# Row sums on one core: the last 64 columns of five loads are sent by two small transfers each

## The chip, the cores and the metric

The kernel runs on one core of a Trainium2 chip; the other cores are idle. The metric is device time in microseconds, and the time of a kernel is the median of its runs. Before the change it was 161.3 us, the median of 3 runs from 161.15 to 161.41.

## What is computed

The input is 64 MiB of float32; each row of 1024 numbers becomes one number.

```python
def setup_inputs():
    batch, seq, dim = 32, 512, 1024
    return {"x": np.random.randn(batch, seq, dim).astype(np.float32)}

def reference(x):
    return np.sum(x, axis=-1).astype(np.float32)
```

## The kernel before

There are 16,384 rows, 128 for each of the 128 partitions of on-chip memory. The first 2,048 rows of the input form one view (`x_a`: partition p holds rows 16p to 16p+15), the other 14,336 another (`x_b`: 112 consecutive rows for each partition). `rows_from` (L131) picks rows `j` to `j+n` of every partition from the one or the other. In both views the rows of a partition are contiguous, so a load of 16 rows reads 64 KB in one stretch for each partition.

All loads are issued by SP (SyncE), in this order: the first 7 rows of `x_b` (L212); then seven whole loads of 16 rows (L214 to L224), of which the first is all of `x_a` and the others are rows 16 to 111 of `x_b`; then what is left of rows 0 to 15, as 6 rows, 2 rows and the last row in two parts of 560 and 464 columns (L227, L228, L236, L237). A load of 16 rows is 8 MiB. The pool `in` has three buffers, so a whole load is issued when the reduction three tiles before it has read its buffer. The first load is moved to the entry of the program, ahead of the start-up barrier; the first two whole loads are held back by explicit dependencies (L222, L224), the first until a small ScalarE instruction has run, the second until the first 7 rows are reduced.

VectorE reduces the first 7 rows and six of the seven whole loads with one instruction each, `tensor_reduce` over 16 rows (L152). The last whole load and the small loads behind it are worked off row by row, by VectorE (`halves`, L166: it adds the two halves of a row and accumulates) and by ScalarE (`act`, L179). The last row's two parts are added by two further `halves` instructions (L241, L242). The row sums gather in the tile `sums`; ScalarE's queue stores two parts of it when the loads are nearly through, and SP stores the last 16 columns at the end (L243).

The function `rows` (L188) issues one load and the instructions that reduce it; the change is made in it and in the loop over `wholes` (L215) that calls it. Each transfer reports its completion on one of eight counters that are used in turn.

Of the kernel before, what the change touches and what calls it, by code (L numbers as in the profile page):

```python
# [100 lines left out]
@with_exitstack  # L101
def kernel(
    ctx: ExitStack,
    tc: tile.TileContext,
    x: bass.AP,
    out: bass.AP,
):
    nc = tc.nc
    nc.at_finalize(issue_first_load_at_entry)
    nc.at_finalize(order_waits)  # L110
    nc.at_finalize(wait_for_the_store_at_the_clear)
    fp32 = mybir.dt.float32
    P = 128
    batch, seq, dim = x.shape
    rows = batch * seq
    J = rows // P
    BIG = 16

    LONG = J - BIG
    rows_in = x.flatten_outer_dims()
    rows_out = out.rearrange("b s -> (b s)")
    x_a = rows_in[: P * BIG].rearrange("(p j) d -> p j d", p=P)
    x_b = rows_in[P * BIG :].rearrange("(p j) d -> p j d", p=P)
    out_a = rows_out[: P * BIG].rearrange("(p j) -> p j", p=P)
    out_b = rows_out[P * BIG :].rearrange("(p j) -> p j", p=P)


    def rows_from(j, n):  # L131
        return x_b[:, j : j + n, :] if j < LONG else x_a[:, j - LONG : j - LONG + n, :]

    last = 0
    FIRST = 7
    pieces = (560, 464)
    LINE = 64

    with (
        tc.tile_pool(name="small", bufs=1) as smallpool,  # L140
        tc.tile_pool(name="in", bufs=3) as inpool,
        tc.tile_pool(name="unread", bufs=4, space=bass.MemoryType.PSUM) as upool,
        tc.tile_pool(name="stage", bufs=1) as stpool,
        tc.manual_schedule(),
    ):


        seed = smallpool.tile([P, LINE // 2], fp32)
        sums = stpool.tile([P, J], fp32)

        def vec(dst, src):
            return nc.vector.tensor_reduce(  # L152
                out=dst, in_=src, axis=mybir.AxisListType.X, op=mybir.AluOpType.add
            )

        def hold(inst, until, reason):
            tc.add_manual_dep(
                inst.ins,
                until.ins.name,
                mybir.DependencyInfo(mybir.DependencyClass.Sync, mybir.DependencyReason.DATA),  # L160
                reason=reason,
            )

        def halves(dst, src):
            n = src.shape[-1] // 2
            return nc.vector.tensor_tensor_reduce(  # L166
                out=src[:, :n],
                in0=src[:, :n],
                in1=src[:, n:],
                scale=1.0,  # L170
                scalar=0.0,
                op0=mybir.AluOpType.add,
                op1=mybir.AluOpType.add,
                accum_out=dst,
            )

        def act(dst, src, n):
            unread = upool.tile([P, dim], fp32)
            nc.scalar.activation(  # L179
                out=unread[:, :n],  # L180
                in_=src,
                func=mybir.ActivationFunctionType.Copy,
                accum_out=dst,
            )

        sums_of = []

        def rows(t, a, n, j, n_act, pairs=False):  # L188
            nv = n - n_act
            block = t[:, a * dim : (a + n) * dim].rearrange("p (n d) -> p n d", d=dim)  # L190
            load = nc.sync.dma_start(out=block, in_=rows_from(j, n))  # L191
            if pairs:
                for q in range(nv):
                    sums_of.append(halves(sums[:, j + q : j + q + 1], block[:, q, :]))
            else:
                sums_of.append(vec(sums[:, j : j + nv], block[:, :nv, :]))
            for q in range(nv, n):
                act(sums[:, j + q : j + q + 1], block[:, q, :], dim)
            return load

        def store(eng, dst, j0, j1):
            return eng.dma_start(out=dst, in_=sums[:, j0:j1])

        nc.vector.memset(seed[:, :1], 0.0)  # L204
        unread = upool.tile([P, dim], fp32)
        ready = nc.scalar.activation(  # L206
            out=unread[:, :1], in_=seed[:, :1], func=mybir.ActivationFunctionType.Copy
        )

        j = last  # L210
        t = inpool.tile([P, BIG * dim + LINE], fp32)
        rows(t, 0, FIRST, j, 0)  # L212
        first = sums_of[-1]
        wholes = [LONG, *range(BIG, LONG, BIG)]  # L214
        for k, at in enumerate(wholes):  # L215
            t = inpool.tile([P, BIG * dim + LINE], fp32)
            if k < len(wholes) - 1:
                load = rows(t, 0, BIG, at, 0)
            else:
                rows(t, 0, BIG, at, 7, pairs=True)  # L220
            if k == 0:
                hold(load, ready, "no second load while the first one's descriptors are made")  # L222
            if k == 1:
                hold(load, first, "no descriptors of later loads while the first ones start")  # L224

        t = inpool.tile([P, BIG * dim + LINE], fp32)
        rows(t, FIRST, 6, j + FIRST, 2, pairs=True)  # L227
        two = rows(t, FIRST + 6, 2, j + FIRST + 6, 1, pairs=True)  # L228
        a = BIG - 1

        j += a
        c, width = pieces
        whole = t[:, a * dim + c : BIG * dim + 2]
        nc.vector.memset(whole[:, width + 1 :], 0.0)  # L234
        part = t[:, a * dim : a * dim + c]
        nc.sync.dma_start(out=part, in_=rows_from(j, 1)[:, 0, :c])  # L236
        nc.sync.dma_start(out=whole[:, :width], in_=rows_from(j, 1)[:, 0, c:])  # L237
        late = "its packets come behind those of the loads"
        hold(store(nc.scalar, out_b[:, BIG:], BIG, LONG), two, late)
        hold(store(nc.scalar, out_a, LONG, J), two, late)  # L240
        halves(whole[:, width : width + 1], part)  # L241
        halves(sums[:, j : j + 1], whole)  # L242
        store(nc.sync, out_b[:, :BIG], 0, BIG)  # L243
# [30 lines left out]
```

## Time and profile before

| | |
|---|---|
| median of 3 runs | 161.3 us (161.15 to 161.41) |
| span of the profiled execution | 159.5 us |
| VectorE busy | 120.6 us, 76% of the span |
| of it `tensor_reduce` of 16 rows | 6 times 17.22 us |
| ScalarE busy | 12.1 us, 8% |
| read from HBM | 67.11 MB, 421 GB/s over the span |
| packets of the transfers | 2160, of which 624 under 512 bytes |
| SP's wait for reductions | 102.2 us |

The span goes from the first to the last instruction of one profiled execution; the device time of a run also holds what lies around it, here 1.8 us. In the rows of the profile, an engine's name stands beside the line of the kernel whose instruction ran (DVE is VectorE, ACT ScalarE, SP SyncE, SPq its queue of instructions). The transfers are carried out by 16 DMA engines, called queues below: each works off its share of the packets of a transfer in order. "DMA share" is their mean busy share, with each packet's time counted in the window in which the packet starts.

### The profile page before, as it was taken

How to read it: one execution, taken by the hardware profiler on the slowest of the kernel's cores; microseconds unless marked ns; L12 is line 12 of the kernel's file. 1: busy time of each engine (PE TensorE's matmuls, PEld its weight loads, DVE VectorE, ACT ScalarE, POOL GpSimd, SP SyncE). 2: the span in 40 equal slices, each digit the busy share in tenths (PEclk: the TensorE clock that was granted, in tenths of full speed). 3: DMA queues.
4: the chain of work that ended last, by engine and by line, in shares of the span. 5: the costliest groups of instructions: out<-in, count | busy, mean ns of one | idle time of the engine just before them, and what ended most of it. 6: DMA issues, size and time to landing. Idle time of an engine off the chain costs nothing.

```text
span 159.5 us, 135 instructions
## 1 busy us (share of the span) xinstructions
DVE 120.6 (76%) x41; ACT 12.1 (8%) x22; POOL 0.2 (0%) x4
## 2 busy tenths in 40 slices
DVE  0029600499995999769996899949999499994955
ACT  3000000000000000000000000000000000003993
POOL 0000000000000000000000000000000000000000
DMA  8899899699699699699699798996996996996993
GB/s 302 388 493 526 362 427 526 296 493 526 263 526 526 263 526 526 263 526 493 296 526 444 345 526 378 411 526 296 493 526 263 526 526 263 526 526 265 425 382 128
DMA packets 2160, 67.18 MB, mean 421 GB/s; under 512 B 624, under 2 KB 752, under 8 KB 880
## 3 DMA queue, kind: packets, MB, share of 16 engines
q1 hardware_dynamic: 1872, 67.12, 97.8%
q10 hardware_dynamic: 288, 0.06, 0.2%
HBM read 67.11 MB, written 0.07 MB: 421 GB/s over the span
## 4 chain that ended last, share of the span: by engine, by line
DMA 71%; DVE 27%; SPq 1%; issue 0%; DVEq 0%
DMA t<-in_x_dram 71%; DVE sums L152 26%; SPq L191 0%; SPq L236 0%; DVE t L166 0%; DVEq L269 0%
## 5 line engine op out<-in xcount | busy, mean ns | idle before, releaser
L152 DVE TENSOR_REDUCE sums<-t 128x16 f32<-128x16384 f32 (+1 forms) x7 | 110.9, 15849 | 32.3 <-DMA t<-in_x_dram 32.3
L179 ACT ACTIVATE unread<-t 128x1024 f32<-128x1024 f32 x10 | 10.1, 1011 | 144.3 <-DMA t<-in_x_dram 144.3
L166 DVE CUSTOM_DVE_ANT_0 t<-t 128x512 f32<-128x512 f32 (+2 forms) x16 | 9.6, 654 | 4.0 <-DMA t<-in_x_dram 4.0
L179 ACT ACTIVATION_READ_ACCUMULATOR unread<-t 128x1 f32 x10 | 1.9, 188 | 0.0
L206 ACT ACT_TABLE_LOAD x1 | 1.3, 1283 | 0.8 <-PEq L258 0.8
L166 DVE DVE_READ_ACCUMULATOR2_ANT sums<- 128x1 f32 x15 | 1.2, 82 | 0.0
L204 DVE MEMSET seed<- 128x1 f32 x1 | 0.1, 59 | 0.8 <-PEq L258 0.8
L206 ACT ACTIVATE unread<-seed 128x1 f32<-128x1 f32 x1 | 0.2, 174 | 0.0
L258 POOL MEMSET const-bfloat16-1.0<- 128x1 bf16 x1 | 0.1, 102 | 0.0
L258 POOL MEMSET const-uint8-127<- 128x1 uint8 x1 | 0.1, 102 | 0.0
L258 POOL MEMSET const-float32-0.0<- 128x1 f32 x1 | 0.1, 99 | 0.2 <-issue 0.2
L258 POOL MEMSET const-float32-1.0<- 128x1 f32 x1 | 0.1, 99 | 0.0
L166 DVE DVE_READ_ACCUMULATOR2_ANT t<- 128x1 f32 x1 | 0.1, 83 | 0.0
L234 DVE MEMSET t<- 128x1 f32 x1 | 0.1, 59 | 0.0
## 6 DMA issues: line engine op xcount, KB each, us to landing
t<-in_x_dram SPq DMA_DIRECT2D x1, 3584.0 KB, 11.0
t<-in_x_dram SPq DMA_DIRECT2D x1, 3072.0 KB, 28.7
t<-in_x_dram SPq DMA_DIRECT2D x1, 1024.0 KB, 30.7
t<-in_x_dram SPq DMA_DIRECT2D x1, 280.0 KB, 31.0
t<-in_x_dram SPq DMA_DIRECT2D x1, 232.0 KB, 31.1
t<-in_x_dram SPq DMA_DIRECT2D x7, 40.7
out_dram<-sums ACTq DMA_DIRECT2D x1, 48.0 KB, 1.6
out_dram<-sums ACTq DMA_DIRECT2D x1, 8.0 KB, 1.6
```

The costliest lines, as they stand in the source:

```text
L152: return nc.vector.tensor_reduce(out=dst, in_=src, axis=mybir.AxisListType.X, op=mybir.AluOpType.add)
L166: return nc.vector.tensor_tensor_reduce(out=src[:, :n], in0=src[:, :n], in1=src[:, n:], scale=1.0, scalar=0.0, op0=mybir.AluOpType.add, op ...
L179: nc.scalar.activation(out=unread[:, :n], in_=src, func=mybir.ActivationFunctionType.Copy, accum_out=dst,)
L204: nc.vector.memset(seed[:, :1], 0.0)
L206: ready = nc.scalar.activation(out=unread[:, :1], in_=seed[:, :1], func=mybir.ActivationFunctionType.Copy)
L234: nc.vector.memset(whole[:, width + 1 :], 0.0)
L258: nc = _bacc.Bacc("TRN2", target_bir_lowering=False, num_devices=1)
```

## The change

For five of the seven whole loads (the second to the sixth), the load itself ends 64 columns early: it takes 16,320 of the 16,384 columns of a partition. The last 64 columns, 256 bytes in each partition, are sent by two small transfers that SP issues right behind it: one over the first partitions (120, 126, 117, 108 and 119 of them) and one over the others (8, 2, 11, 20 and 9). The first and the last whole load and the loads of fewer rows are left as they were, and no instruction of VectorE or ScalarE is changed; a reduction of a cut load waits for three transfers in place of one.

```diff
+    EDGE = 64
...
-        def rows(t, a, n, j, n_act, pairs=False):
+        def rows(t, a, n, j, n_act, pairs=False, head=0):
             nv = n - n_act
             block = t[:, a * dim : (a + n) * dim].rearrange("p (n d) -> p n d", d=dim)
-            load = nc.sync.dma_start(out=block, in_=rows_from(j, n))
+            src = rows_from(j, n).rearrange("p n d -> p (n d)")
+            cut = n * dim - (EDGE if head else 0)
+            load = nc.sync.dma_start(out=t[:, a * dim : a * dim + cut], in_=src[:, :cut])
+            if head:
+                at = slice(a * dim + cut, (a + n) * dim)
+                nc.sync.dma_start(out=t[:head, at], in_=src[:head, cut:])
+                nc.sync.dma_start(out=t[head:, at], in_=src[head:, cut:])
...
         wholes = [LONG, *range(BIG, LONG, BIG)]
+        heads = {1: 120, 2: 126, 3: 117, 4: 108, 5: 119}
         for k, at in enumerate(wholes):
             t = inpool.tile([P, BIG * dim + LINE], fp32)
             if k < len(wholes) - 1:
-                load = rows(t, 0, BIG, at, 0)
+                load = rows(t, 0, BIG, at, 0, head=heads.get(k, 0))
```

## The prediction

> **What bounds the kernel now.** I read the chain of waits in order of time first, because it names what released each step. Its last part:
>
> ```profile
> 107.58 17.23 DVE sums L152
> ...
> 124.82 0.33 SPq L191
> ...
> 126.16 31.13 DMA t<-in_x_dram
> 157.30 0.02 issue
> 157.32 0.40 DVE t L166
> ```
>
> The columns are start, length and what ran. The end is set by the landing of the last piece of input at 157.30 us; behind it come a 0.40 us add and the last store, 2.19 us up to the end of the span at 159.49. The chain steps back from that landing to its issue, then to the reduction that freed the buffer; that is no proof of a wait that matters, for the load was asked for 31 us before it landed. So I asked next whether the transfers ever ran dry, with windows of one load each (last two columns: DMA share, GB/s):
>
> ```profile
> 69.00:88.30 19.30, 17.22 (x2) 0.00 (x0) 0.00 (x0) 1.00 1.00 435
> 88.30:107.60 19.30, 17.24 (x2) 0.00 (x0) 0.00 (x0) 1.00 1.00 435
> ```
>
> They don't: share 1.00, 435 GB/s, which is 27.2 bytes per ns for each of 16 queues. VectorE needs 17.22 of the 19.3 us of a load and waits the other 2.1. SP waits most of all, always to ask early:
>
> ```profile
> SPq L191 <- DVE sums L152: 102.2, 6, 17.2
> ```
>
> The kernel is bound by its transfers from 1.0 us to the end, and what counts is the queue that finishes last. How far apart the 16 queues run shows in narrow windows at the moments when each begins its first, and its forty-ninth, 64 KB packet; a packet counts where it starts, and 328 GB/s in 0.2 us is one packet:
>
> ```profile
> 9.90:10.10 0.20, 0.00 (x0) 0.00 (x0) 0.00 (x0) 1.00 0.76 328
> 10.10:10.30 0.20, 0.00 (x0) 0.00 (x0) 0.00 (x0) 1.00 4.55 1966
> 10.30:10.50 0.20, 0.00 (x0) 0.00 (x0) 0.00 (x0) 1.00 5.31 2294
> 10.50:10.70 0.20, 0.00 (x0) 0.00 (x0) 0.00 (x0) 1.00 1.52 655
> ...
> 125.90:126.10 0.20, 0.00 (x0) 0.00 (x0) 0.00 (x0) 1.00 0.77 328
> 126.10:126.30 0.20, 0.00 (x0) 0.00 (x0) 0.00 (x0) 1.00 4.59 1966
> 126.30:126.50 0.20, 0.00 (x0) 0.00 (x0) 0.00 (x0) 1.00 5.34 2294
> 126.50:126.70 0.20, 0.00 (x0) 0.00 (x0) 0.00 (x0) 1.00 1.52 655
> ```
>
> That is 1, 6, 7 and 2 packets, at 10 us and again 116 us later: each queue keeps the lateness it got at the start. The whole spread is some 0.5 to 0.6 us, and two queues come about 0.15 us behind the rest (a window from 10.46 to 10.62 us is empty). If the work were dealt out so that all ended together, the end could come about 0.25 us earlier (half the spread), as long as the dealing itself cost nothing.
>
> **Which queue gets what.** The edit takes 128 pieces of 256 bytes out of each of five loads and sends them as ten small transfers. Before, the page counts 2160 packets for 15 transfers: 15 x 128 of data and 15 x 16 of four bytes, so every transfer went in equal shares of 8 rows, with one closing packet each, to all 16 queues. 120, 8, 126, 2, 117, 11, 108, 20, 119 and 9 rows have no sixteenth. I assume that equal shares stay the rule, on the largest number of queues up to 16 that divides the rows, always from the first queue on: 15, 8, 14, 2, 13, 11, 12, 10, 7 and 9 queues. Added up over the five loads, the queues then carry, in place of 40 pieces each: 58, 58, 57, 57, 57, 57, 57, 40, 39, 38, 36, 35, 26, 17, 8 and 0. [...]
>
> **The price of a piece.** No 256-byte read is in the trace, so I bound it. Below: bytes alone, 256 / 27.2 = 9.4 ns. Above: the two stores that are made of small packets, read with windows on the queues alone:
>
> ```profile
> q1 hardware_dynamic: 144, 0.01, 10.3%
> ...
> q10 hardware_dynamic: 144, 0.05, 49.4%
> ```
>
> The first is 64-byte packets in a window of 0.90 us: 0.103 x 16 x 0.90 / 144 = 10.3 ns each. The second is 384-byte packets in 0.37 us: 0.494 x 16 x 0.37 / 144 = 20.3 ns. In between, 256 bytes come to 16.3 ns, and four bytes to 8.4. Neighbouring packets of a queue overlap a little: the page gives the loads' queue 97.8% of 16 x 159.5 us, 156.0 us a queue, and a queue has on average only from 1.1 to 156.7 us and a tenth more for the last store; 0.3 us over some 117 packets is 2 ns. I take 14.5 ns for a piece and 7 ns for a closing packet, between the bounds and near the upper rows.
>
> **The sum.** What a queue saves in the five loads is 40 x 9.4 = 376 ns. The five queues with 57 pieces pay 57 x 14.5 = 827 ns and ten closing packets, 70 ns: 521 ns more than before (at 9.4 ns and free closing packets, 160; at 16.3 and 8.4, 637). A queue with no piece gains 376. The latest of the seven loaded queues decides. Which queues are late the trace doesn't say; if the seven were drawn at random, one of the two late ones is among them with 1 - (9 x 8)/(16 x 15) = 0.70, and the end moves by 0.52 us; else by 0.15 less, 0.37. If the loaded ones are the seven earliest, some 0.35 us ahead of the last, it still moves by 0.17. Together about +0.5 us.
>
> **Costs I put at nothing.** Ten issues on SP, 0.33 to 0.44 us each by the rows of the loads' issues: SP is idle for them, and a load is asked for some 20 us before its queue needs it (asked 66.87, landed 107.55, its forerunner 88.3); without that cover they would add 0.7 us a load. The built order adds waits: completion counters come in a ring of eight, so with 25 transfers in place of 15 the second small transfer of the third, fourth and fifth cut load waits for the main part of a load two earlier to land, about 2 us after SP gets there. Behind it in SP's queue stands the next whole load, which waits for a reduction some 17 us later anyway. VectorE's reductions wait for three landings in place of one; SP's rows of such a wait are 17 ns each, inside VectorE's 2.1 us of idle. The instructions of VectorE and ScalarE and the last four loads are unchanged, so the 2.19 us behind the last landing stay, as do the 1.8 us between the span and the median. The profiled execution goes from 159.5 to 160.0 us, the median of 161.3 to 161.8.
>
> **Rivals.** *The late queues are relieved.* If the queues with few pieces are just those that set the end, and the loaded seven are over 0.9 us ahead of them (0.52 + 0.376), the end comes up to 0.376 us earlier: about 160.95. Against it: the windows show a spread of at most 0.6 us. For it: an unprofiled execution may start less evenly than this one. *Even dealing.* If any number of rows is spread over all 16 queues, each gets 40 pieces: 40 x 14.5 + 70 - 376 = +0.27 us, 161.57. The equal shares of before speak for neither. *Pieces in the way of others.* Until now each queue wrote only its own partitions. Shares of 17 rows or 9 fall elsewhere, and if a piece holds up the queue that owns the partition while it itself waits, each costs another 9.4 ns on the loaded queues: +0.52 + 57 x 9.4 ns = +1.05, 162.35. No view of before shows a transfer in another's way. [...] *It doesn't reach the end:* the pieces hide in gaps between packets that the records do not show; 161.3.
>
> **How the numbers follow.** Forecast 0.58 (own range 161.4 to 162.1), relief 0.12, even dealing 0.12, pieces in the way 0.13, no effect 0.05. Within 0.2% of before, which is 0.32 us and about what a measurement can tell from no change, lie 0.10 of the forecast, 0.07 of even dealing and 0.04 of no effect: 0.21. Faster is the relief alone, 0.12. The rest, 0.67, is slower. The range 161.2 to 162.3 leaves out the relief below and half of the collisions above, 0.18.
>
> **What would show it.** The packets: equal shares add 640 pieces and 15+8+14+2+13+11+12+10+7+9 = 101 closing packets, 2901 in all; even dealing adds 160 closing ones, 2960. The landing of the last piece should move from 157.30 to about 157.8, with VectorE's wait for it longer; narrow windows where the seventh whole load begins should show the 16 starts drawn out from 0.6 to about 1 us, some earlier than before, half of them later. A stretch below 430 GB/s in the middle of the loads would mean that a wait has emptied the queues, which I have excluded; a spread that shrinks would make the forecast wrong.

## The result and the profile after

The changed kernel takes 162.03 us (median of five runs) where the kernel before took 161.19 in the same comparison. The ratio is 1.0046 with a 95% interval of 1.0032 to 1.006, so the change costs 0.5 to 1.0 us. Three runs of this document were 2 to 3.5 us slower than the rest of their kernel: one of these five, at 165.44 us, which is left out of the ratio and of the spans below, and two of the twelve of `after_less` (an experiment below), at 163.66 and 163.87 us, which are in its ratio and widen its interval. The forecast was 161.8, in a range of 161.2 to 162.3.

The chain of waits of the changed kernel in order of time, its last part (start, length, what ran):

```profile
126.83 30.75 DMA t<-in_x_dram
157.58 0.04 issue
157.62 0.40 DVE t L167
```

The last piece lands at 157.58 us instead of 157.30. The span of this execution grows with it, from 159.5 to 159.8. That is only part of the loss. Each run has its device time and its span, and the part outside the span has grown as well: 2.13 to 2.17 us in every run of the changed kernel, 1.74 to 1.84 in every run of the kernel before that went with the experiments. The forecast had put the whole loss inside the span.

Inside the span things went as foreseen. The transfers did not run dry in the middle of the loads (windows of one load each; last two columns DMA share and GB/s):

```profile
69.00:88.30 19.30, 17.22 (x1) 0.00 (x0) 0.00 (x0) 1.00 1.01 435
88.30:107.60 19.30, 17.22 (x1) 0.00 (x0) 0.00 (x0) 1.00 1.01 435
```

The page's line on the packets, and below it the narrow windows where the queues begin their first 64 KB packet and where they begin the seventh whole load:

```profile
DMA packets 2901, 67.18 MB, mean 420 GB/s; under 512 B 1365, under 2 KB 1493, under 8 KB 1621
```

```profile
9.90:10.10 0.20, 0.00 (x0) 0.00 (x0) 0.00 (x0) 1.00 0.76 328
10.10:10.30 0.20, 0.00 (x0) 0.00 (x0) 0.00 (x0) 1.00 4.55 1966
10.30:10.50 0.20, 0.00 (x0) 0.00 (x0) 0.00 (x0) 1.00 6.07 2622
10.50:10.70 0.20, 0.00 (x0) 0.00 (x0) 0.00 (x0) 1.00 0.76 328
...
125.90:126.10 0.20, 0.00 (x0) 0.00 (x0) 0.00 (x0) 1.00 0.77 328
126.10:126.30 0.20, 0.00 (x0) 0.00 (x0) 0.00 (x0) 1.00 0.77 328
126.30:126.50 0.20, 0.00 (x0) 0.00 (x0) 0.00 (x0) 1.00 4.06 1697
126.50:126.70 0.20, 0.00 (x0) 0.00 (x0) 0.00 (x0) 1.00 4.87 2034
126.70:126.90 0.20, 0.00 (x0) 0.00 (x0) 0.00 (x0) 1.00 2.45 1020
```

2901 packets is the number that equal shares on as many queues as divide the rows give; even dealing would have made 2960. At 10 us the 16 queues start as 1, 6, 8 and 1 packets, close to the 1, 6, 7 and 2 of before. At 126 us one starts early and one 0.2 us later, some five start between 126.3 and 126.5, six between 126.5 and 126.7 and three behind 126.7 (256-byte pieces make up the odd GB/s). By the packets' own start times in the two traces, the 0.5 us in which all 16 start have become 0.84 us (126.05 to 126.89), where the kernel before still has 0.5: the uneven dealing pulled them apart.

VectorE's instructions for line 153, the reductions, show what else the edit added:

```profile
L153 DVE TENSOR_REDUCE sums<-t x7: 7619/17219/17220, 11.0 to 127.5; 128x16 f32<-128x16384 f32 x6, 128x7 f32<-128x7168 f32 x1
L153 DVEq EVENT_SEMAPHORE  x5: 49/50/50, 49.9 to 127.3; - x5
```

Each of the five reductions that wait for three landings is preceded by an instruction of its own that only waits, 50 ns each in VectorE's idle time. The kernel before has none of them at its reductions, so the list of VectorE's instructions has become longer by five. That matters for another reason than their 50 ns, as the experiments show.

### The profile page after: what moved, and what is told of

It is laid out like the page before. It is cut to its first block, busy times and chain, and to the rows that moved or that the text cites. A ratio compares the mean times of both kernels' runs of the same rounds, so it can differ in the third digit from the quotient of the medians.

```text
span 159.8 us, 151 instructions
## 1 busy us (share of the span) xinstructions
DVE 120.6 (75%) x41; ACT 12.1 (8%) x22; POOL 0.2 (0%) x4
## 2 busy tenths in 40 slices
DMA packets 2901, 67.18 MB, mean 420 GB/s; under 512 B 1365, under 2 KB 1493, under 8 KB 1621
## 4 chain that ended last, share of the span: by engine, by line
DMA 81%; DVE 16%; SPq 1%; issue 0%; DVEq 0%
DMA t<-in_x_dram 81%; DVE sums L153 16%; SPq L194 1%; SPq L197 0%; SPq L244 0%; DVE t L167 0%; SPq L198 0%; DVEq L153 0%; DVEq L277 0%
```

## The experiments

Twelve kernels ran, each at least five times, against the kernel before. The table has the medians: span, device time minus span ("outside"), device time, all in us; "VectorE" is how many instructions of VectorE its trace records more than the trace of the kernel before, which has 50. Each comparison's own runs of the kernel before had a median of 161.19 to 161.26; in the experiments their span was 159.4 to 159.5 and 1.76 to 1.79 us lay outside.

| kernel | pieces | VectorE | span | outside | time |
|---|---|---|---|---|---|
| changed kernel | 640, uneven | +5 | 159.85 | 2.15 | 162.03 |
| `e_even` | 640, even, ten transfers | +5 | 159.6 | 2.15 | 161.80 |
| `e_one` | 640, even, five transfers | +5 | 159.6 | 2.18 | 161.80 |
| `e_lump` | 640, on seven queues | +5 | 160.2 | 2.20 | 162.40 |
| `e_idle` | 10 | 0 | 159.4 | 1.78 | 161.23 |
| `e_wait` | 10 | +5 | 159.5 | 2.21 | 161.63 |
| `e_extra` | 640 on top, even | 0 | 160.0 | 1.77 | 161.76 |
| `e_pad` | none | +5 | 159.8 | 2.18 | 161.97 |
| `e_less` | none | -6 | 159.4 | 1.78 | 161.21 |
| `e_pad1` | none | +1 | 159.6 | 1.78 | 161.38 |
| `e_pad15` | none | +15 | 159.8 | 1.79 | 161.62 |
| `after_less` | 640, uneven | -1 | 159.75 | 1.78 | 161.54 |
| `after_pad35` | 640, uneven | +40 | 160.5 | 1.81 | 162.31 |

### Is it the dealing, or the program?

The first theory after the result, A, was that the queues cost about half and a longer program of SP, with ten transfers more to issue, the rest. The rival, B, left everything to the queues. Four kernels went together.

`e_even` deals the same pieces evenly:

```diff
-        heads = {1: 120, 2: 126, 3: 117, 4: 108, 5: 119}
+        heads = {1: 112, 2: 112, 3: 112, 4: 112, 5: 112}
```

> All five cut loads send their 640 pieces as 112+16 rows, so that every one of the 16 queues gets 40 of them, with as many transfers (ten) as the changed kernel. Theory A (the loss is half in the queues, half in a longer program): the span grows by 40 x 14.1 ns + 10 x 6 ns - 376 ns = 0.25 us to about 159.75, the time outside the span stays at the changed kernel's 2.15 us, median about 161.9. Theory B (the whole loss comes from the queues that carry 57 pieces): even dealing gives back most of it, median about 161.4.

Measured: 161.80 us, 1.0041 of before (1.0027 to 1.0055), span 159.6, outside 2.15. The 14.1 ns for a piece and 6 ns for a closing packet, here and in what follows, fit the records of the changed kernel's trace: 18 and 9 ns, less the 3 to 4 ns by which neighbouring packets of a queue overlap there. (In the kernel before, too: a whole load is eight packets of 2.419 us and one of 9 ns for a queue, 19.36 us by their records, and the first packets of two loads start 19.33 us apart.) In the span even dealing gives back most of the loss (0.25 of 0.4 us); outside it, nothing. The windows at the seventh whole load of this kernel:

```profile
126.10:126.30 0.20, 0.00 (x0) 0.00 (x0) 0.00 (x0) 1.00 0.19 39
126.30:126.50 0.20, 0.00 (x0) 0.00 (x0) 0.00 (x0) 1.00 7.21 3026
126.50:126.70 0.20, 0.00 (x0) 0.00 (x0) 0.00 (x0) 1.00 5.55 2343
126.70:126.90 0.20, 0.00 (x0) 0.00 (x0) 0.00 (x0) 1.00 0.00 0
```

All 16 queues start within 0.4 us: nothing has pulled them apart.

`e_lump` makes the dealing more uneven:

```diff
-        heads = {1: 120, 2: 126, 3: 117, 4: 108, 5: 119}
+        heads = {1: 119, 2: 119, 3: 119, 4: 119, 5: 119}
```

> All five cut loads are 119+9, so that seven queues get 90 pieces each, two get five and seven get none; ten transfers. Both theories: the seven queues carry 90 x 14.1 + 10 x 6 - 376 = 0.95 us more than before (57 pieces: 0.49), so the last landing comes 0.4 to 0.5 us later than in the changed kernel: span 160.2 to 160.4, median 162.4 to 162.6. If the dealing doesn't set the end, the median stays at 162.0. The count of packets is 2160 + 640 + 5 x (7 + 9) = 2880.

Measured: 162.40 us, 1.0071 (1.0058 to 1.0084), span 160.2, outside 2.20, 2880 packets. The span is 0.35 us longer than the changed kernel's, at the low end of what was expected. Its windows, 0.4 us wide, in which 164 GB/s is one packet:

```profile
125.70:126.10 0.40, 0.08 (x1) 0.00 (x0) 0.00 (x0) 1.00 3.09 1312
126.10:126.50 0.40, 0.00 (x0) 0.00 (x0) 0.00 (x0) 1.00 0.39 164
126.50:126.90 0.40, 0.00 (x0) 0.00 (x0) 0.00 (x0) 1.00 0.04 8
126.90:127.30 0.40, 0.00 (x0) 0.00 (x0) 0.00 (x0) 1.00 1.43 555
127.30:127.70 0.40, 0.00 (x0) 0.00 (x0) 0.00 (x0) 1.00 1.56 665
```

Nine queues begin the load by 126.5, then none for 0.4 us, then seven: 119 rows went to seven queues, in five loads running always to the same seven. For 119 rows this shows what the forecast had to assume. The packets agree with it in sum: 2901 in the changed kernel, 2880 here and 2960 in `e_even`. Which seven of the sixteen queues it is no record here shows. The nine also show that relief is real: eight of them start before 126.1, where in the kernel before only one did.

`e_one` sends each edge by a single transfer of 128 rows:

```diff
             if head:
...
                 nc.sync.dma_start(out=t[:head, at], in_=src[:head, cut:])
-                nc.sync.dma_start(out=t[head:, at], in_=src[head:, cut:])
...
-        heads = {1: 120, 2: 126, 3: 117, 4: 108, 5: 119}
+        heads = {1: 128, 2: 128, 3: 128, 4: 128, 5: 128}
```

> Each of the five edges is sent by one transfer of 128 rows in place of two: 40 pieces for every queue as in the even dealing, but five more transfers than before instead of ten. Span 159.5 + 40 x 14.1 + 5 x 6 - 376 ns = 159.7. Theory A: the time outside the span lies between 1.7 and 2.15 us by how much of the program went, median 161.4 to 161.85. Theory B: median 161.4.

Measured: 161.80 us, 1.0034 (1.0021 to 1.0046), outside 2.18. Five issues less on SP change nothing against `e_even`.

`e_idle` adds SP's issues without cutting a load:

```diff
+        def spare():
+            n = len(idles) * LINE
+            idles.append(nc.sync.dma_start(out=idle[:1, n : n + LINE], in_=x_b[:1, 0, :LINE]))
...
                 load = rows(t, 0, BIG, at, 0)
+                if k > 0:
+                    spare()
+                    spare()
```

> The loads are whole, as before; SP issues ten transfers of one row of 256 bytes into a tile that nobody reads, two behind each of the five loads. One queue of 16 gets ten packets and ten closing packets (up to 0.2 us, which counts only if it is the last). Theory A: the span is 159.5 to 159.7, the time outside it 2.15 us, median 161.6 to 161.8. Theory B: the time outside the span is as before (1.7 us), median 161.2 to 161.4.

Measured: 161.23 us, 0.9995 (0.9986 to 1.0003), outside 1.78. Ten more transfers on SP cost nothing, in the span or outside it. Theory A's second half falls, and B with it: all four cut kernels have 2.15 to 2.20 us outside, however evenly they deal and however many transfers they use.

### What do cut loads add outside the span?

Two things are common to the cut kernels and absent from `e_idle`: 640 pieces (theory D) and five more instructions on VectorE (theory C).

`e_wait` is `e_idle` with the reductions waiting for the idle transfers:

```diff
-                    spare()
-                    spare()
+                    for _ in range(2):
+                        hold(sums_of[-1], spare(), "one more landing to wait for")
```

> As the run with ten idle transfers of one row (whole loads, nothing cut), but the reductions of the five loads wait for two of them as well, as the changed kernel's wait for its small transfers: five more waiting instructions on VectorE, no pieces. Theory C (the 0.38 us outside the span, common to all four kernels with cut loads, come from VectorE's longer list of instructions or its waits): outside 2.15 us, span 159.4 to 159.5, median 161.6. Theory D (they come with the 640 pieces): outside 1.78, median 161.25.

Measured: 161.63 us, 1.0026 (1.0016 to 1.0036); span 159.5, outside 2.21.

`e_extra` leaves the loads whole and reads their edges a second time, into a tile that nothing reads, so that the pieces come without the waits:

```diff
+                if k > 0:
+                    col = slice((k - 1) * LINE, k * LINE)
+                    src = x_b[:, at + BIG - 1, dim - LINE :]
+                    nc.sync.dma_start(out=spare[:112, col], in_=src[:112])
+                    nc.sync.dma_start(out=spare[112:, col], in_=src[112:])
```

> The five loads stay whole and their last 64 columns are read once more, by two transfers over 112 and 16 rows, into a tile that nobody reads: 640 pieces dealt evenly, ten transfers, no change on VectorE. In the span every queue pays 40 pieces and ten closing packets without saving a byte: 40 x 14.1 + 60 = 0.62 us, span about 160.1 (at 18 ns a piece 160.3). Outside the span: 1.78 us by theory C, 2.15 by theory D; median 161.9 or 162.3.

Measured: 161.76 us, 1.0035 (1.0023 to 1.0047); span 160.0, outside 1.77. Theory D is out. In the span the pieces cost 0.56 us, the two medians apart; with 0.06 for the closing packets that is 12.5 ns a piece. The interval, 0.37 to 0.76 us, allows 8 to 17 ns. The same working from the times of `e_even`, `e_one` and `e_lump`, less what they have more outside the span and with the 0.376 us of saved bytes added, gives 11.5 to 12.2 ns. So some 12 ns is an estimate on which four runs agree, less than the 14.1 expected and the 14.5 of the forecast.

`e_pad` has neither pieces nor waits, only five memsets:

```diff
+                if k > 0:
+                    nc.vector.memset(pad[:, k : k + 1], 0.0)
```

> The kernel before with five more memsets of one column on VectorE, one behind each of five reductions, and no change to a load. They lie in VectorE's idle time, so the span stays at 159.5. If the length of VectorE's list of instructions is what shows outside the span, outside is 2.15 us and the median 161.6; if only waits for several landings do it, or the pieces, outside is 1.78 and the median 161.25.

Measured: 161.97 us, 1.0048 (1.0036 to 1.006), outside 2.18. So five memsets do it as well as five waits. The span was a miss: 159.6 to 160.2 in its six runs, against an expected 159.5. In the profiled execution the last landing is at 157.70. Its trace shows the place but not the cause: 43 of the 896 packets of 64 KB, spread from 75 to 141 us, take more than 2.47 us, up to 2.68, where in the kernel before none takes over 2.45. With one memset in all (`e_pad1`, below) no packet is that slow and with fifteen (`e_pad15`) a single one, so it does not go with the number of memsets.

### A cost per instruction, a step, or a place?

`after_less` takes instructions away from the changed kernel elsewhere on VectorE, in the last whole load, ahead of idle time; `e_less` does the same to the kernel before. The expectations count five fewer; the traces record six fewer (49 for 55, and 44 for 50), because a wait at the line of the pairs goes too:

```diff
-                for q in range(nv):
+                both = 3 if n == BIG else 0
+                if both:
+                    sums_of.append(vec(sums[:, j : j + both], block[:, :both, :]))
+                for q in range(both, nv):
```

> The changed kernel, with the last whole load's first three VectorE rows reduced by one instruction in place of three pairs: five instructions fewer on VectorE, as many as the cut loads' waits had added; VectorE still ends that load before the next one lands. Theory C (the length of VectorE's list costs 0.38 us outside the span): outside falls back to 1.78 us, span stays 159.8, median 161.6. If the waits themselves or the pieces do it, outside stays 2.15 and the median 162.0.

> The kernel before with the same five instructions fewer on VectorE. If the cost outside the span grows with each instruction (0.38 us for five), outside falls to 1.4 us and the median to 160.85; if it is a step that lies between the kernel before and five more, outside stays 1.78 and the median 161.25.

Measured: `after_less` 161.54 us, outside 1.78, span 159.75, against 161.21 for the kernel before beside it (ratio 1.0037, 1.0006 to 1.0068). With the list one short of its old length, the cut loads cost 0.33 us by the medians (0.1 to 1.1 by the interval), all of it in the span. `e_less` 161.21 us, 0.9995 (0.9985 to 1.0005), outside 1.78: no cost per instruction, and nothing to be won by a shorter list.

`e_pad1` and `e_pad15` are `e_pad` with one memset in all, and with three behind each of five reductions.

> The kernel before with one more memset on VectorE. By a cost per instruction outside grows by 0.08 to 1.86 us; by a step it is 1.78 or 2.15. Span 159.5.

> The kernel before with fifteen more memsets on VectorE, three behind each of five reductions. By a cost per instruction outside is 2.9 us; by one step it is 2.15, as with five. Span 159.5, or up to 0.4 more if the memsets disturb the transfers.

Measured: `e_pad1` 161.38 us, 1.0006 (0.9994 to 1.0019), outside 1.78. `e_pad15` 161.62 us, 1.0017 (1.0006 to 1.0029), outside 1.79. So it is no step either: fifteen more cost nothing outside. But the span of `e_pad15` is longer, by 0.4 us in the medians and 0.35 in the profiled executions, and its trace shows most of that at the very end. The instructions of the closing barrier, by engine, with first and last start: first the kernel before, then `e_pad15`.

```profile
L269 SPq DRAIN  x3: 7/7/7, 158.4 to 158.7; - x3
L269 PEldq DRAIN  x2: 8/8/8, 0.8 to 158.8; - x2
L269 DVEq DRAIN  x2: 19/219/419, 157.4 to 158.7; - x2
...
L269 DVEq EVENT_SEMAPHORE  x2: 21/21/21, 158.6 to 159.4; - x2
...
L269 POOLq EVENT_SEMAPHORE_RANGE_CLEAR  x1: 92/92/92, 159.2 to 159.2; - x1
```

```profile
L273 SPq DRAIN  x3: 7/7/7, 158.5 to 158.8; - x3
L273 PEldq DRAIN  x2: 8/8/8, 0.9 to 158.9; - x2
...
L273 DVEq DRAIN  x2: 132/252/373, 157.5 to 159.3; - x2
...
L273 DVEq EVENT_SEMAPHORE  x2: 21/21/21, 158.8 to 159.8; - x2
...
L273 POOLq EVENT_SEMAPHORE_RANGE_CLEAR  x1: 93/93/93, 159.6 to 159.6; - x1
```

Before, VectorE's last drain starts with those of the other engines, 0.11 us behind VectorE's wait at 158.64. In `e_pad15` that wait starts at 158.76 but the drain only at 159.29, some 0.4 us behind the other engines' drains, and the closing clear comes behind it (159.6, not 159.2; the last add starts only 0.12 us later). VectorE stood still for 0.4 us in front of that drain, between the 63rd and the 64th instruction that its trace records. This gave theory E: one place in VectorE's list at which it stands still. It lies behind the recorded part of the list before, 50 instructions; with fifteen more it comes just ahead of the last instruction of the span, with five more some eight instructions behind it, which is where no record reaches.

`after_pad35` tests that by moving the place into idle time:

```diff
                 load = rows(t, 0, BIG, at, 0, head=heads.get(k, 0))
+                if k > 0:
+                    for q in range(7 * k - 7, 7 * k):
+                        nc.vector.memset(pad[:, q : q + 1], 0.0)
```

> The changed kernel with 35 more memsets on VectorE, seven behind each reduction of a cut load (about 0.3 us in idle time of 2 us). Theory E (there is one place in VectorE's list, some instructions behind the end of the list of the kernel before, where it stands still for 0.4 us; five more put it behind the last instruction of the span, fifteen more just ahead of it): forty more than in the kernel before put it among the row halves of the last whole load, where VectorE has 1.9 us of idle: outside falls to 1.78 us, the span stays 159.8, median 161.6, 0.4 faster than the changed kernel with 35 instructions fewer. If long lists cost outside the span whatever their length, or once they pass a length, outside is 2.15 or more and the median 162.0 or more.

Measured: 162.31 us, 1.0063 (1.0049 to 1.0077). Of theory E one half holds: outside is 1.81, back from 2.15 with forty instructions more than before. The standstill itself is not seen. The 63rd instruction recorded on VectorE is the row half that starts at 150.28, and the 64th starts at 150.89 (lines of the timeline: start, length, what ran):

```profile
149.67 0.69 DVE L167 CUSTOM_DVE_ANT_0 t<-t 128x512 f32<-128x512 f32 x1
150.28 0.69 DVE L167 CUSTOM_DVE_ANT_0 t<-t 128x512 f32<-128x512 f32 x1
150.89 0.68 DVE L167 CUSTOM_DVE_ANT_0 t<-t 128x512 f32<-128x512 f32 x1
```

All row halves of that load follow each other every 0.61 us, as in the kernel before. So either VectorE does not stand still there in this kernel, or it does so in the idle time on either side of these rows.

The half on the time is a miss: the span is 160.5, not 159.8. The queues' rows of its trace, in the window from 133 to 135 us, point to a reason, beside the end of its chain of waits:

```profile
q1 hardware_dynamic: 16, 1.05, 122.7%
q14 instruction: 1, 0.01, 1.0%
```

```profile
126.73 31.42 DMA t<-in_x_dram
158.15 0.03 issue
158.18 0.40 DVE t L167
```

One packet of 8 KB is an instruction fetch, in the middle of the loads, at 133.78 to 134.09 us. The data packet that starts just as it ends, at 134.09, takes 2.99 us by its record, where all others of its size take 2.41 to 2.46, and the last piece lands at 158.15, 0.57 us later than in the changed kernel. The two delays agree, so the fetch probably went through a queue that could not spare it; no run takes the fetch away to test that. In the changed kernel's trace no fetch lies inside the span. In that of `e_pad15` one comes at 159.94, 0.65 us behind the end of the standstill.

## Why the prediction was right, point by point

- *What bounds the kernel* held: 435 GB/s in the middle of the loads, and the last landing sets the end of the span (157.58 us, 2.2 us ahead of it, as before).
- *Which queue gets what* held to the packet in sum, 2901, and in the seven queues apart in `e_lump`. That every transfer begins with the same queue, on which the counts of 57 and 58 pieces rest, is the forecast's assumption, and nothing read from the runs shows it for transfers of different sizes; shown are the same seven queues for the five transfers of 119 rows, and starts drawn out to 0.84 us in the changed kernel.
- *The price of a piece* was a little high: some 12 ns by four runs (12.5 by `e_extra`, whose interval also allows 14.5), against 14.5. The overlap of neighbouring packets, taken as 2 ns, is 3 to 4 ns in the records. Of the seven loaded queues the five with 57 pieces have, by that assumption, nine closing packets and not ten, 7 ns less; that changes nothing.
- *The sum* was +0.5 us in the queues. Measured in the span: 0.28 in the last landing of the profiled executions, 0.35 to 0.4 in the medians, 0.33 with the list's cost removed (`after_less`). That lies between the forecast's 0.17 for seven early queues and 0.52 for a late one among them; with 12 ns a piece and 6 ns a closing packet the same sum gives 0.37. How late the queues start differs between executions: in the window from 10.50 to 10.70 us two start in the kernel before, one in the changed kernel, none in `e_lump` and `e_even`. Whether the late ones are the same queues each time is not shown.
- *Costs I put at nothing*: SP's ten issues cost nothing (`e_idle`), and the waits on the counters emptied no queue (435 GB/s; the second small transfers wait three times, 1.3 us at most, not 2). The step that failed is "as do the 1.8 us between the span and the median". It named VectorE's extra waits and priced them by their length, 17 ns where they took 50, which idle time covers; that they lengthen VectorE's list by five instructions, to where the list costs 0.37 us outside the span, was in no row of before. That is almost half of the loss, and with six instructions fewer the time was 161.54 (`after_less`).
- *Rivals.* Relief is real for the relieved queues (`e_lump`), but the loaded ones lose more. Even dealing is not what the transfers did (2901 packets, not 2960); made to, in `e_even`, they still cost 0.1 to 0.2 us in the span. Pieces in the way of others, +1.05, did not show: in `e_lump` the relieved queues came early (eight started before 126.1 us, one in the kernel before), where 40 pieces in the way of a queue, at 9.4 ns each, would have cancelled the 376 ns that it saves; and the loaded ones lost no more than their own pieces, 11.5 ns each. Which queue writes which partitions no record here shows.

So the mechanism of the queues was right, with a term that was too large (0.5 for about 0.35), and a second cost of the same size was missing (0.37). That 162.03 still fell inside the range is partly luck: the upper part of the range was kept for pieces in the way of others, which did not show, and the missing cost came to lie there.

## What to carry to other kernels

When every queue is busy from start to end, small pieces for balancing must cost less than the imbalance: here 40 pieces of 256 bytes save a queue 0.38 us of bytes and cost it about 0.5, and transfers of 120, 8, 126 and other numbers of rows that sixteen doesn't divide were dealt unevenly by themselves (2901 packets, not 2960). Compare device time with span in every run: a cost that no row of the profile shows can sit between them, here 0.37 us. Kernels with idle instructions added tell whether it comes from the program itself, but try several numbers of them: here five showed it, while one and fifteen did not. A wait for several landings was also an instruction in a list here, five of 50 ns in the changed kernel.

## What was not expected of the hardware

In these kernels the device time outside the span depends on how many instructions VectorE's list has, and not evenly. Five more than before cost 0.37 to 0.44 us there, in six kernels, whether they are waits or memsets; six fewer, one fewer, one more, fifteen more and forty more cost nothing there. Two to four more, and six to fourteen, were not tried.

With fifteen more, VectorE is seen to stand still for 0.4 us inside the span, in front of its 64th recorded instruction (0.53 us from the start of its wait to the drain, where the kernel before has 0.11). That the 0.37 us of the changed kernel are the same standstill, behind the end of the records, is inferred from these numbers. With forty more there is no standstill at that place and no cost outside the span. So theory E is not proven, and what makes VectorE stand still is open.

With forty more, an instruction fetch of 8 KB (q14) lies inside the span, at 133.78 us, and there one data packet takes 2.99 us, over 0.5 us longer than the others; the kernels with one, five and fifteen more memsets and with six instructions fewer have none in the span. Whether the place has to do with a fetch no run here shows, for in neither trace do the two fall together (133.78 and 150.9 us in `after_pad35`, 159.94 and 159.3 us in `e_pad15`).
